# Adding partial outputs of the MLPs into y by accumulating DMAs from staging tiles, instead of by VectorE

## The chip, the core and the metric

The kernel runs on one core of a Trainium2 chip. The core has five engines with a queue of instructions each: TensorE (PE; its weight loads are listed apart as PEld), VectorE (DVE), ScalarE (ACT), GpSimd (POOL) and SyncE (SP), which here only issues DMAs. Sixteen DMA engines move the data. Matmuls write to PSUM; everything else lies in SBUF. The metric is the time of one execution on the device, in microseconds.

## The reference

A backbone of two layers over 512 latent tokens and 256 context tokens of width 1024. Each layer has a mixer (layer 0: neighbourhood attention beside spatial gating; layer 1: bidirectional retention) and then a gated MLP with a depthwise convolution over the tokens; around every sub-layer stand an RMS norm with a shift and a scale ahead of it, and a norm, a gate and the residual behind it. The change concerns the MLP:

```python
def conv_ffn(h, w_in, conv_w, conv_b, w_out):
    a = dwconv3(h @ w_in, conv_w, conv_b)          # w_in: 1024 x 5632
    gate, up = jnp.split(a, 2, axis=-1)
    return (jax.nn.silu(gate) * up) @ w_out        # w_out: 2816 x 1024

# per layer, latent stream; layer 0 also for the context stream
h = modulate(rmsnorm(x, norm_g[i, 2]), sh2, sc2)
x = x + g2 * rmsnorm(conv_ffn(h, ...), norm_g[i, 3])
```

All of it is float32.

## The kernel before

Tokens are cut into tiles of 128: tiles 0 to 3 are latent, 4 and 5 context. Layer 0 works on all six, layer 1 on the four latent ones. A float32 product is made of three passes: each operand is split into a high and a low part (`split`: ScalarE writes the high one, VectorE subtracts to get the low one, line 65), and `mm3` (lines 88 to 90) does high x high, high x low and low x high. Weights come from HBM in units of 512 KB by DMAs of SP's queue into three raw tiles, and are split into a ring of weight tiles (`unit`, `slot`).

The MLP (`ffn`) runs over 22 feature tiles j. For each, `project` multiplies the input weights of gate and up (units `f..`) with the tokens, into PSUM tiles `pf` (latent) and `pc` (context); `gated` does the convolution, the SiLU and the product on ScalarE and VectorE (lines 1148 to 1157) and splits the result into `g`. Two feature tiles are one group (`GF = 2`), and there are 11 groups. Behind every second feature tile the output projection of the group before is done: `w_out` loads and splits two units `fo..`, and `out_group` runs through the pieces. A piece is one half (512 columns) of one token tile: six matmuls into a PSUM tile `wf` (the two tiles with tag "B" are used in turn), and then the sum into y, 128 x 1024 float32 per token tile in SBUF, where layer 0's rows show it as `yf`. The first group is copied into y by ScalarE (line 389); every later one is added by VectorE (line 391):

```python
if first:
    self.S.copy(y[t][:, o], ps)
else:
    self.V.tensor_tensor(out=y[t][:, o], in0=ps, in1=y[t][:, o], op=ALU.add)
```

So a group has 12 pieces in layer 0 and 8 in layer 1. The last two groups are done by `out_last`: group A of the two early token tiles (`wf0A`, `wf1A`), then group B of these (`wf0B`), and both groups in one piece for the other token tiles (`wf0C`); B and C use the four PSUM tiles of tag "A". Behind the last piece of a token tile, `final` runs norm, gate and residual (`residual`), in which GpSimd does the roots. `ada_half` works in the background on the shifts, scales and gates of later sub-layers: GpSimd zero-fills two sums `acc` (line 199), SP loads a row into each, VectorE adds weighted rows (line 208).

Each engine takes its instructions in order. The order is fixed when the program is built, by a scheduler that places instructions by its own estimate of when they can start, and that turns every use of a tile into the needed waits on semaphores.

Of the kernel before, what the change touches and what calls it, by code (L numbers as in the profile page):

```python
# [36 lines left out]
class Trunk:  # L37
# [42 lines left out]
    def phase(self, ctx, name, extra):  # L80
        self.xp = ctx.enter_context(self.tc.tile_pool(name=name, bufs=1))
        self.extra = extra
        self.turn = 0
        return self.xp

# [42 lines left out]
    def ada_first(self, q, pool, native, tag):  # L128
        """shift and scale of a quarter of the features, latent and context, for the first sub-layer; a step per unit"""
        S, V, T = self.S, self.V, self.T  # L130
# [125 lines left out]

# [1 line left out]
    def rsq(self, w, name):  # L258
# [9 lines left out]
    def ssq(self, src, name, n):  # L268
        """mean square over the row, a half (n) at a time"""
        ss = self.sst.get(name)  # L270
        if ss is None:
            ss = self.sst[name] = self.bp.tile([P, 2], F32, name=f"ss{name}", tag="ss", bufs=8)
        junk = self.t2k(f"j{name}{n}", BF16)
        self.S.activation(junk, src, AF.Square, scale=1.0 / 32, accum_out=ss[:, n : n + 1])  # L274
# [23 lines left out]
    def residual(self, t, y, gate, src, last, name, xt):  # L298
        """y (final) -> x += rmsnorm(y) * gate; then x normed into y's place."""
        V = self.V  # L300
        self.load(xt, src)
        hv = [slice(0, 512), slice(512, 1024)]
        for n, h in enumerate(hv):
            self.ssq(y[:, h], f"y{name}{t}", n)
        for h in hv:
            V.tensor_tensor(out=y[:, h], in0=y[:, h], in1=gate[:, h], op=ALU.mult)
        r = self.rms(f"y{name}{t}")
        for n, h in enumerate(hv):
            V.scalar_tensor_tensor(out=xt[:, h], in0=y[:, h], scalar=r, in1=xt[:, h], op0=ALU.mult, op1=ALU.add)  # L309
            if last:  # L310
                self.load(self.out[t * P : (t + 1) * P, h], xt[:, h])
            else:
                self.ssq(xt[:, h], f"x{name}{t}", n)
        if last:
            return
        self.load(self.xd[t], xt)
        r = self.rms(f"x{name}{t}")
        V.tensor_scalar(out=y[:, hv[0]], in0=xt[:, hv[0]], scalar1=r, scalar2=None, op0=ALU.mult)
        self.S.activation(y[:, hv[1]], xt[:, hv[1]], AF.Copy, scale=r)
# [11 lines left out]
    def build_h(self, chunk, xn, ab, name):  # L331
        """chunk 2: context tokens, chunks 0 and 1: latent halves."""
        s = 1 if chunk == 2 else 0
# [23 lines left out]
    def hcols(self, t):  # L357
        """stationary views of token tile t: k -> (hi, lo)"""
        if t >= 4:
            c = slice((t - 4) * P, (t - 3) * P)  # L360
            return lambda k: (self.hc[0][:, k, c], self.hc[1][:, k, c])
        c = slice(t * P, (t + 1) * P)
        return lambda k: (self.hl[0][:, k, c], self.hl[1][:, k, c])

    def proj_t(self, ps, w, stream, half=None):
        """ps[feat, tokens] += w^T h, w a stationary unit"""
        h = self.hc if stream else self.hl
# [6 lines left out]

# [1 line left out]
    def out_pieces(self, feats, wo, y, toks, first, final, name, tag="B"):  # L376
        """y[t] (+)= sum over the group's feature tiles, one closure per half token tile;
        feats: list of (hi, lo)[feat, tokens]"""

        def piece(t, n):  # L380
# [7 lines left out]
            if first:  # L388
                self.S.copy(y[t][:, o], ps)
            else:  # L390
                self.V.tensor_tensor(out=y[t][:, o], in0=ps, in1=y[t][:, o], op=ALU.add)  # L391
# [9 lines left out]
    def out_last(self, A, B, y, toks, early, final, name):  # L401
        """the last two groups (feats, wo): group A of the early tokens, group B of these, both for the others"""
        e, o = toks[:early], toks[early:]
        self.out_group(*A, y, e, False, None, f"{name}A")
        if callable(B):
            B = B()
        self.out_group(*B, y, e, False, final, f"{name}B", "A")
        self.out_group(A[0] + B[0], A[1] + B[1], y, o, False, final, f"{name}C", "A")

    def finisher(self, gates, src, ab, name, xts, last=False):  # L410
        """per finished token tile: the residual update, then the next sub-layer's input once a chunk is there"""
        done = {}
# [20 lines left out]

# [1 line left out]
    def sgu(self, y, xn):  # L435
# [178 lines left out]
    def project_pair(self, j, pr):  # L614
        """q, k, v of two heads, transposed; returns the steps"""
        w = [self.unit(self.a["hyb_qkv"][(4 * i + j) * P : (4 * i + j + 1) * P], f"w{'qkv'[i]}{j}") for i in range(3)]
# [56 lines left out]
    def bias_tiles(self, h, hd):  # L673
        """8 x (relative bias, or the mask) of the three kinds of query tile"""
        G, ap = self.G, self.ap
# [13 lines left out]
    def score(self, h, b, pr, hd):  # L689
        """softmax of one query tile (b = 4: both context tiles), queries on partitions"""  # L690
        S, V, T, ap = self.S, self.V, self.T, self.ap
# [63 lines left out]
    def weigh(self, h, b, pr, hd):  # L755
        """keys onto partitions, and after a head's last tile the weighted values"""
        S, V, T = self.S, self.V, self.T
# [35 lines left out]

# [1 line left out]
    def retention(self, y, final):  # L795
        S, V, T, G, a = self.S, self.V, self.T, self.G, self.a
        KS = float(np.float32(P) ** np.float32(-0.5))
        with ExitStack() as ctx:
# [19 lines left out]
            def decay(h):  # L818
                """powers of the two decays: within a chunk, of the keys, of the queries, of a chunk"""
                d = hd[h]  # L820
# [35 lines left out]
            def k_nat(h):  # L856
                """keys onto partitions, decayed towards the end and towards the start of their chunk:
                [token tile of the chunk, direction, (context, latent), dk]"""
                d = hd[h]
# [20 lines left out]
            def states(h):  # L880
                """sums of key x value before (forwards) and behind (backwards) each chunk: [chunk, direction, dv]"""
                d = hd[h]
# [216 lines left out]

# [1 line left out]
    def ffn(self, l, y, final):  # L1101
# [192 lines left out]
def stat(w):  # L1294
    """[1024, n] -> tiles [n/128 * 128, 8 * 128]: row p of tile j holds w[k*128+p, j*128+c] as (k, c)"""
    n = w.shape[1]
# [3 lines left out]
def mov(w, width):  # L1300
    """[1024, n] -> units of 1024 / width row blocks by width columns"""
    n, g = w.shape[1], 1024 // width
# [3 lines left out]
def cols(v):  # L1306
    """[m, 1024-multiple] -> [128, ...] one column per block of 128"""
    return v.reshape(-1, P).T
# [52 lines left out]
```

## Time and profile before

| | us |
|---|---|
| median of 3 runs | 1920.09 (1918.94 to 1925.68) |
| span of the profiled execution | 1922.2 |
| TensorE busy | 1856.5 |
| VectorE busy | 1274.3 |
| ScalarE busy | 811.5 |
| GpSimd busy | 166.0 |
| MLP of layer 0, groups with adds | about 540 to 960 |
| MLP of layer 1, to the end | about 1545 to 1922 |

The span is from the first to the last instruction of one profiled execution; that execution's own time is not listed apart from its span, which lies inside the range of the runs. In a row of a group of instructions stand the line, the engine, the operation, what it writes and reads, the shape, the count, then after the bar the busy time, the mean in ns, and the idle time of the engine just before, with what ended it. In a row of a list of instructions stand the start, the duration, the engine, the line and the operation, and in brackets the idle time before. `A <- B` in a list of waits is A waiting for B: total, number, longest. Line numbers in rows of the profile are those of the kernel before; in the changed kernel lines 84 to 390 stand one further down, and later ones five.

### The profile page before, as it was taken

The page shows a single profiled execution, that of the slowest core. Times are in us where ns is not written, and L with a number is a line of the kernel's source. Part 1 is how long each engine was busy: PE and PEld are TensorE (multiplying, and loading weights), DVE is VectorE, ACT ScalarE, POOL GpSimd, SP SyncE. Part 2 cuts the span into 40 slices and gives each one's busy share as a digit, 9 for nine tenths or more (in the row PEclk, how much of TensorE's full clock was granted, in tenths as well). Part 3 has the DMA queues.
Part 4 walks back from the last instruction along what each step waited for, and adds up shares of the span by engine and source line. Part 5 has one row for each costly group of instructions (what it writes and reads, how often), then busy time and mean ns, then how long its engine had stood idle before and what let it go on. Part 6 is the DMA issues. An engine that isn't in the chain of part 4 may idle for free. (4 is left out here: it accounts for less than half of the span.)

```text
span 1922.2 us, 26580 instructions
## 1 busy us (share of the span) xinstructions
PE 1856.5 (97%) x10544; PEld 1567.6 (82%) x10544; DVE 1274.3 (66%) x2103; ACT 811.5 (42%) x1340; POOL 166.0 (9%) x249
## 2 busy tenths in 40 slices
PE   7998989989999999999989999999999899999998
PEld 4886867678888888888879889988999787888886
DVE  4844688679698755555577666676655696566565
ACT  6533545665432323222365434443444454333322
POOL 1102222130000000000021110011001100000001
PEclk9999999999999999999999999999999999999999
DMA  7323332143444311122334313331421254332222
GB/s 287 113 97 104 94 103 90 47 143 116 139 143 132 100 65 47 64 66 66 110 114 132 126 53 109 115 105 46 131 67 56 99 185 157 99 99 92 95 66 88
DMA packets 58301, 199.88 MB, mean 104 GB/s; under 512 B 7200, under 2 KB 8736, under 8 KB 58176
## 3 DMA queue, kind: packets, MB, share of 16 engines
q1 hardware_dynamic: 58176, 198.17, 31.5%
q8 instruction: 83, 1.36, 0.3%
q14 instruction: 42, 0.34, 0.1%
HBM read 187.66 MB, written 10.49 MB: 103 GB/s over the span
## 5 line engine op out<-in xcount | busy, mean ns | idle before, releaser
L208 DVE SCALAR_TENSOR_TENSOR acc<-ar,cs,acc 128x512 f32<-128x512 f32 x256 | 189.2, 759 | 21.3 <-DMA ar<-in_adaw 8.9
L391 DVE TENSOR_TENSOR yf<-wf,yf 128x512 f32<-128x512 f32 x160 | 110.0, 689 | 53.0 <-PE wf L90 52.7
L1148 ACT ACTIVATE cv<-pf,cw 128x512 f32<-128x512 f32 x88 | 67.4, 766 | 38.3 <-PE pf L90 38.2
L64 ACT ACTIVATE g<-cv 128x768 fp32r<-128x768 f32 (+1 forms) x44 | 32.6, 740 | 120.0 <-DVE cv L1157 120.0
L1149 DVE SCALAR_TENSOR_TENSOR cv<-pf,cw,cv 128x511 f32<-128x511 f32 x88 | 65.6, 745 | 16.9 <-ACT cv L1148 16.8
L1152 DVE SCALAR_TENSOR_TENSOR cv<-pf,cw,cv 128x511 f32<-128x511 f32 x88 | 65.8, 747 | 1.7
L1156 ACT ACTIVATE cv<-cv 128x768 f32<-128x768 f32 (+1 forms) x44 | 32.3, 734 | 39.4 <-DVE cv L1152 39.4
L199 POOL MEMSET acc<- 128x512 f32 x32 | 16.8, 527 | 336.8 <-DVE al L65 236.1
L1148 ACT ACTIVATE cv<-pc,cw 128x256 f32<-128x256 f32 x44 | 24.8, 564 | 49.4 <-PE pc L90 25.6
L65 DVE TENSOR_TENSOR g<-cv,g 128x768 fp32r<-128x768 f32 (+1 forms) x44 | 36.2, 822 | 12.6 <-ACT g L64 11.8
L1157 DVE TENSOR_TENSOR cv<-cv,cv 128x768 f32<-128x768 f32 (+1 forms) x44 | 36.1, 821 | 0.5
L960 DVE SCALAR_TENSOR_TENSOR of<-rx,e,of 128x256 f32<-128x256 f32 x64 | 28.9, 478 | 8.4 <-PE rx L90 7.9
L980 POOL TENSOR_SCALAR rrr<-rmv 128x2 f32<-128x2 f32 x16 | 3.1, 193 | 363.1 <-DVE rmv L977 363.1
L751 ACT ACTIVATE sc<-sc,sst 128x512 f32<-128x512 f32 x32 | 23.1, 721 | 23.1 <-DVE sc L742 22.6
L279 POOL TENSOR_SCALAR wye<-ssye 128x1 f32<-128x1 f32 x4 | 2.7, 673 | 348.3 <-ACT jye L274 348.3
L391 DVE TENSOR_TENSOR yr<-wr,yr 128x512 f32<-128x512 f32 x40 | 27.5, 688 | 5.2 <-PE wr L90 4.8
L279 POOL TENSOR_SCALAR wyc<-ssyc 128x1 f32<-128x1 f32 x6 | 4.2, 699 | 291.5 <-ACT jyc L274 291.5
L870 ACT ACTIVATE kd<-kn,e 128x256 fp32r<-128x256 f32 x32 | 14.0, 475 | 35.7 <-PE kn L867 31.5
L65 DVE TENSOR_TENSOR rv<-rn,rv 128x512 fp32r<-128x512 f32 x24 | 16.5, 686 | 18.1 <-ACT rv L64 18.1
L1149 DVE SCALAR_TENSOR_TENSOR cv<-pc,cw,cv 128x255 f32<-128x255 f32 x44 | 21.1, 479 | 9.8 <-ACT cv L1148 9.8
L986 DVE TENSOR_SCALAR on<-of,rmv,rrr 128x256 f32<-128x256 f32 x32 | 18.1, 603 | 11.8 <-POOL rrr L983 11.8
L695 PE MATMUL s<-ka,q 128*128 128x256 f32 x80 | 24.0, 321 | 1.3 <-ACT sc L708 1.1
(2836 smaller groups left out, 6928.2 us busy)
## 6 DMA issues: line engine op xcount, KB each, us to landing
ar<-in_adaw SPq DMA_DIRECT2D x96, 512.0 KB
xd<-xd SPq DMA_DIRECT2D x8, 512.0 KB
xn<-in_x SPq DMA_DIRECT2D x6, 512.0 KB
ngr<-in_norm_g SPq DMA_DIRECT2D x12, 256.0 KB
xb<-in_x SPq DMA_DIRECT2D x6, 512.0 KB
xd<-xb SPq DMA_DIRECT2D x6, 512.0 KB
xc<-xd SPq DMA_DIRECT2D x6, 512.0 KB
xd<-xc SPq DMA_DIRECT2D x6, 512.0 KB
```

The lines of the kernel that those rows point to most:

```text
L64: self.S.activation(hi, src, AF.Copy)
L65: self.V.tensor_tensor(out=lo, in0=src, in1=hi.bitcast(F32), op=ALU.subtract)
L208: V.scalar_tensor_tensor(out=acc[s], in0=raw[:, kk * 512 : kk * 512 + 512], scalar=self.cs[:, 8 * s + k : 8 * s + k + 1], in1=acc[s], op0= ...
L391: self.V.tensor_tensor(out=y[t][:, o], in0=ps, in1=y[t][:, o], op=ALU.add)
L695: T.matmul(out, q[:, cols], keys(ka), start=True, stop=False)
L751: S.activation(sc, sc, AF.Exp, bias=st[:, 0:1], scale=-1.0, accum_out=st[:, 1:2])
L960: V.scalar_tensor_tensor(out=d["o"][:, t], in0=ps[:, n], scalar=d["e"][n][:, 386 + i : 387 + i], in1=d["o"][:, t], op0=ALU.mult, op1=ALU.add,)
L1148: S.activation(d, s, AF.Identity, scale=w1, bias=b)
L1149: V.scalar_tensor_tensor(out=d[:, 1:n], in0=s[:, 0 : n - 1], scalar=w0, in1=d[:, 1:n], op0=ALU.mult, op1=ALU.add)
L1152: V.scalar_tensor_tensor(out=d[:, 0 : n - 1], in0=s[:, 1:n], scalar=w2, in1=d[:, 0 : n - 1], op0=ALU.mult, op1=ALU.add)
L1156: S.activation(act[0], act[0], AF.Silu)
L1157: V.tensor_tensor(out=act[0], in0=act[0], in1=act[1], op=ALU.mult)
```

## The change

For the two MLPs (`self.stage` is set where the pool of tiles is named "ffnp..."), a piece that is neither of the first group nor finishing its token tile is copied by ScalarE from PSUM into a staging tile `yp` of 128 x 512 float32, of which there are four, and then a DMA issued by GpSimd adds that tile to the half of y in SBUF. Pieces of the first group, pieces that finish a token tile, and the mixers stay as they were. The rest of the difference is comments.

```diff
@@ phase
         self.extra = extra
         self.turn = 0
+        self.stage = name.startswith("ffnp")
         return self.xp
@@ out_pieces
             if first:
                 self.S.copy(y[t][:, o], ps)
+            elif not final and self.stage:
+                part = self.xp.tile([P, 512], F32, name=f"yp{name}{t}{n}", tag="yp", bufs=4)
+                self.S.copy(part, ps)
+                self.G.dma_start(y[t][:, o], part, accum_op=ALU.add)
             else:
                 self.V.tensor_tensor(out=y[t][:, o], in0=ps, in1=y[t][:, o], op=ALU.add)
```

VectorE before, in a middle group of layer 0 (feature tiles 10 and 11). In a name `wf01040_6842` stand the layer (0), the first feature tile (10), the token tile (4), the half (0) and a buffer number; `fo012l` is the low part of output weight 12.

```order
L391 TENSOR_TENSOR yf004_4746<-wf01040_6842,yf004_4746 128x512
L1152 SCALAR_TENSOR_TENSOR cv0113_6817<-pf0113_6785,cw0_4004,cv0113_6817 128x511
L391 TENSOR_TENSOR yf004_4746<-wf01041_6850,yf004_4746 128x512
L1157 TENSOR_TENSOR cv0013_6810<-cv0013_6810,cv0113_6817 128x768
L391 TENSOR_TENSOR yf005_4763<-wf01050_6858,yf005_4763 128x512
```

These adds, twelve to a group, are gone from VectorE. ScalarE in the changed kernel, at the same group:

```order
L393 COPY ypf01040_6945<-wf01040_6938 128x512
L393 COPY ypf01041_6955<-wf01041_6948 128x512
L393 COPY ypf01050_6965<-wf01050_6958 128x512
L64 ACTIVATE g0013_6922<-cv0013_6906 128x768
L393 COPY ypf01051_6975<-wf01051_6968 128x512
L393 COPY ypf01000_6985<-wf01000_6978 128x512
L393 COPY ypf01001_6995<-wf01001_6988 128x512
L393 COPY ypf01010_7005<-wf01010_6998 128x512
L393 COPY ypf01011_7015<-wf01011_7008 128x512
L393 COPY ypf01020_7025<-wf01020_7018 128x512
L393 COPY ypf01021_7035<-wf01021_7028 128x512
L393 COPY ypf01030_7045<-wf01030_7038 128x512
```

Before, ScalarE had the split of `g` here and none of the copies; behind the row of the eleventh piece follow the split of output weight 12 and the twelfth copy. Each copy waits for its matmuls, and from the fifth on for the DMA that read its staging tile four copies earlier.

GpSimd in the changed kernel, where the first accumulates of layer 0 begin (`acc1..` are the sums that `ada_half` fills with zeros for layer 1):

```order
L200 MEMSET acc101_5014 128x512
L394 DMA yf004_4746<-ypf0240_5179 128x512
L200 MEMSET acc110_5457 128x512
L394 DMA yf004_4746<-ypf0241_5189 128x512
L200 MEMSET acc111_5460 128x512
L394 DMA yf005_4763<-ypf0250_5199 128x512
L394 DMA yf005_4763<-ypf0251_5209 128x512
```

Before, only the zero-fills stood in this queue; now each DMA waits there for its copy, and two zero-fills, which wait for VectorE, stand between the first three DMAs. The order of the matmuls changes only by small exchanges of neighbours, and SP's queue not at all.

## The prediction

> **What bounds the kernel now.** The page's busy times come first, then the waits of TensorE inside the two MLP stretches, then the stretches themselves.
>
> ```profile
> PE 1856.5 (97%) x10544; PEld 1567.6 (82%) x10544; DVE 1274.3 (66%) x2103; ACT 811.5 (42%) x1340; POOL 166.0 (9%) x249
> L391 DVE TENSOR_TENSOR yf<-wf,yf 128x512 f32<-128x512 f32 x160 | 110.0, 689 | 53.0 <-PE wf L90 52.7
> ```
>
> TensorE (PE) is busy 97% of the span; a pipelined PE can be busy and still be slow, so this alone proves nothing. The second row is the work that the change moves: 160 adds of 0.689 us, and what ends VectorE's idle time before them is TensorE (52.7 of 53.0 us). VectorE waits for the matmuls, not they for it. The question is then whether TensorE ever waits for VectorE here. Its waits from 440 to 970 us (MLP of layer 0), the whole list:
>
> ```profile
> PE pf L89 <- DVE hl1b L65: 0.4, 1, 0.4
> PE pf L88 <- ACT hl0b L64: 0.2, 1, 0.2
> PE wf L88 <- DVE yf L391: 0.2, 1, 0.2
> ```
>
> and from 1545 us to the end (MLP of layer 1):
>
> ```profile
> PE wf L88 <- ACT yf L389: 0.3, 1, 0.3
> ```
>
> Together 1.1 us. The stretches (columns: window, length, busy time of PE, weight loads, VectorE, ScalarE, GpSimd, then granted clock, DMA share, GB/s):
>
> ```profile
> 640.00:760.00 120.00, 119.85 (x620) 99.89 (x619) 75.16 (x110) 34.57 (x45) 0.53 (x1) 1.00 0.24 79
> 760.00:880.00 120.00, 120.00 (x635) 101.95 (x634) 66.03 (x90) 34.34 (x43) 0.00 (x0) 1.00 0.21 66
> 1600.00:1700.00 100.00, 100.00 (x432) 80.65 (x433) 61.37 (x78) 35.30 (x44) 0.00 (x0) 1.00 0.33 106
> ```
>
> Matmuls follow each other without a gap at full clock, VectorE has 40 to 45% of its time free, ScalarE some 70%, GpSimd nearly all, and the DMA engines two thirds. So the matmuls bound both MLPs, and a gain from unloading VectorE has no place to appear.
>
> **The pace of the pieces.** The rest hangs on one clock, that of a piece (half a token tile, six matmuls):
>
> ```profile
> 759.81 0.69 DVE L391 TENSOR_TENSOR yf<-wf,yf 128x512 f32<-128x512 f32 x1 [0.70 <-PE wf L90]
> 761.20 0.69 DVE L391 TENSOR_TENSOR yf<-wf,yf 128x512 f32<-128x512 f32 x1 [0.70 <-PE wf L90]
> 762.60 0.69 DVE L391 TENSOR_TENSOR yf<-wf,yf 128x512 f32<-128x512 f32 x1 [0.70 <-PE wf L90]
> ```
>
> One piece each 1.40 us ((762.60 - 759.81) / 2). A group has 12 pieces in layer 0, 8 in layer 1.
>
> **Term 1, the moved evacuation: 0.** Out go 168 adds (8 x 12 + 8 x 8 in the middle groups, 4 + 4 of the early tokens in the last): 168 x 0.689 = 116 us of VectorE. In come 168 ScalarE copies. A copy of the same shape from PSUM stands in the trace, that of the first group:
>
> ```profile
> L389 ACT COPY yf<-wf x12: 568/588/588, 490.8 to 506.5; 128x512 f32<-128x512 f32 x12
> ```
>
> 168 x 0.588 = 99 us of ScalarE, whose 811.5 become some 910: cover enough. Two PSUM buffers serve the pieces, so a buffer must be free 1.40 us after its piece ends; 0.59 does that as 0.69 did, and this first group already runs so. What can stand ahead of a copy on ScalarE is a split of a gated tile (between copies 3 and 4) or of an output weight (between 11 and 12):
>
> ```profile
> L64 ACT ACTIVATE g<-cv 128x768 fp32r<-128x768 f32 x14 | 11.9, 849 | 46.0 <-DVE cv L1157 46.0
> L64 ACT ACTIVATE fo012h<-fo012r 128x1024 fp32r<-128x1024 f32 x1 | 1.1, 1062 | 10.8 <-PE wf L90 10.8
> ```
>
> 0.85 + 0.59 = 1.44 us is 0.04 past the limit, at most; behind copy 11 no piece of the group needs a buffer any more. From 0 to 16 x 0.04 = 0.6 us: I take 0. Weights and gated tiles that ScalarE prepares behind its copies are used a whole pair of feature tiles later, and the loads have room too; SP's queue itself waits for buffers:
>
> ```profile
> SPq L50 <- DVE fo012l L65: 17.2, 1, 17.2
> ```
>
> **Term 2, the staging ring: 0, and the place where it can go wrong.** There are four staging tiles, so copy k waits until the DMA of piece k-4 has landed. Call L the time from the end of a copy to the landing. Counted from a group's start, copy 2 ends at 2 x 1.40 + 0.59 = 3.39, its DMA lands at 3.39 + L, copy 6 ends no earlier than 3.98 + L, lands at 3.98 + 2L, copy 10 ends at 4.57 + 2L, and piece 12 needs the PSUM buffer of piece 10 at 11 x 1.40 = 15.40. So a group of 12 loses nothing up to **L = 5.4 us**. In a group of 8, piece 8 needs copy 6 at 9.80: nothing up to L = 5.8.
>
> No DMA of GpSimd and no accumulating one is in this trace, so L is bounded by the nearest DMAs of SP in the chain of waits (start, duration from release to landing):
>
> ```profile
> 1563.97 3.68 DMA acc<-in_adab_row
> 1574.95 4.49 DMA fo11r<-in_ffn_out
> 1588.60 3.32 DMA f105r<-in_ffn_in
> ```
>
> A row of 2 KB takes 3.68 us, 512 KB of weights 3.32 to 4.49. The accumulate moves 256 KB, reads source and target, both on the chip. I take L = 4.1, the middle of the outer two; below 5.4. Ends: 3.3 if it behaves like the fastest; 8 if issue by GpSimd and reading the target twice over each add about as much as half a load does. L = 7 costs 4.57 + 14 - 15.40 = 3.2 us in each of 8 groups of 12 and 3.98 + 7 - 9.80 = 1.2 in each of 8 groups of 8: +35. L = 8 costs 8 x 5.2 + 8 x 2.2 = +59.
>
> Then the rate r, one DMA after another:
>
> ```profile
> q1 hardware_dynamic: 58176, 198.17, 31.5%
> ```
>
> 198.17 MB in 31.5% of 1922.2 us is 327 GB/s with all engines at work; 0.262 MB take 0.80 us, twice that if the target's reading counts fully (1.60), and 2.4 where weights take a third of the engines (share 0.33 above). A group of 12 bears 1.99 + L + 5r + 0.59 <= 15.40, with L = 4.1 that is r <= 1.74. I take 0.8 to 1.6: no stall. At r = 2.4 it is 3.3 us x 8 = +26; groups of 8 bear it (1.99 + 4.1 + 2.4 + 0.59 = 9.1 < 9.8).
>
> [...]
>
> GpSimd must also be free to issue. The longest VectorE instruction in these stretches is
>
> ```profile
> 1580.55 1.24 DVE fo11l L65
> ```
>
> If an issue had to sit out one of these, L would be 4.1 + 1.2 = 5.3, still just inside. [...]
>
> **Term 3, GpSimd's queue: +2.** A zero-fill of GpSimd stands between the first accumulates of layer 0, and waits for VectorE:
>
> ```profile
> 546.97 0.53 POOL L199 MEMSET acc<- 128x512 f32 x1 [22.30 <-DVE al L65]
> 549.79 0.53 POOL L199 MEMSET acc<- 128x512 f32 x1 [2.30 <-DVE al L65]
> 542.86 0.68 DVE L391 TENSOR_TENSOR yf<-wf,yf 128x512 f32<-128x512 f32 x1
> ```
>
> The second and third accumulate (due at 544.8 and 546.2, if copies start when the first add did, at 542.86) are held to 547.5 and 550.3, so the third lands at 554.4. Copy 7, due at 542.86 + 6 x 1.40 = 551.3, ends at 555.0 instead, and piece 9, due at 542.86 + 7 x 1.40 = 552.7, starts 2.3 us late. From 0, if VectorE with fewer adds before it frees those tiles sooner, to 3; once: +2. The other fills stand between groups, behind the last accumulate of the one and ahead of the next.
>
> **Term 4, the ends of the layers: 0.** The last VectorE adds now wait for landings of the early tokens' accumulates:
>
> ```profile
> 1892.37 0.68 DVE L391 TENSOR_TENSOR yf<-wf1A,yf 128x512 f32<-128x512 f32 x1
> 1897.73 0.69 DVE L391 TENSOR_TENSOR yf<-wf1B,yf 128x512 f32<-128x512 f32 x1 [0.67 <-PE wf1B L90]
> 1903.01 0.68 DVE L391 TENSOR_TENSOR yf<-wf1B,yf 128x512 f32<-128x512 f32 x1
> 1917.59 1.42 DVE L309 SCALAR_TENSOR_TENSOR xe<-yf,ye3r,xe 128x512 f32<-128x512 f32 x2 [0.85 <-POOL ye3r L260]
> ```
>
> First copy done at 1892.37 + 0.59, landed 4.1 later at 1897.1, before 1897.73. The tail that follows is VectorE's own and keeps its length: from -2.8 (four adds gone, 4 x 0.69) to +2.
>
> **Sum.** 0 + 0 + 2 + 0 = +2 us. The profiled execution's span is 1922.2, 2.1 above the median of 1920.09 and inside the runs (1918.94 to 1925.68), so I add to the median: **1922 us**. With the small bounds (-2.8 - 1.1 below; 0.6 + 3 + 2 above) and the runs' own spread, 1914 to 1929 for this case.
>
> **The rivals.** A measurement of this kernel tells about 0.5%, 9.6 us, from no change.
>
> 1. *The accumulates land too late* (slower). The place is ScalarE's copy, waiting for a staging tile with the PSUM buffer in its hand; it decides from L = 5.4 and costs +35 at L = 7: 1955. For it: nothing like this DMA is in the trace, and 4.49 is near. Against: 256 KB on the chip is half of the load that takes 3.3 to 4.5. Chance 0.17.
> 2. *They land one by one too slowly* (slower): the doubled reading beside weights, or GpSimd's issue itself, r = 2.4: +26, 1946; it decides from 1.74. For it: 1.60 is close below. Against: the share of 0.21 to 0.33 leaves most engines free. Chance 0.11.
> 3. *VectorE's relief shortens the changes between layers* (faster). At most the 1.1 us of waits, 2.8 at each of two layer ends, and some of the 4.8 us that TensorE lacks here:
>
> ```profile
> 980.00:1010.00 30.00, 25.21 (x170) 22.26 (x169) 22.19 (x35) 20.07 (x45) 7.37 (x12) 0.98 0.26 95
> ```
>
> That makes 1909 to 1914; against it, the work there is norms and transposes, none of which is moved. Chance 0.05.
>
> That the change does nothing is excluded: the order shows adds replaced by copies and DMAs.
>
> **How the numbers follow.** The forecast has 0.67, rivals 0.17 + 0.11 and 0.05. Faster 0.05, same 0.67, slower 0.28. The range goes down to 1913 and up to rival 1's 1955, which leaves out about 0.15.
>
> **What would show it.** Right: TensorE's waits in 520 to 880 stay near 1 us, ScalarE's copies of "yp" are released by PE, the accumulates land 3.3 to 5.4 us after their copies, VectorE's busy time falls by 116 us. Rival 1 or 2: copies released by DMA, matmuls "wf" waiting for copies, 2 to 4 us in each group of layer 0 and little in layer 1; landings a constant time late for the first, later with each piece for the second. Rival 3: the stretch 980 to 1010 shorter. The prediction is wrong if GpSimd is what the copies' DMAs wait for.

## The result and the profile after

| | before | after |
|---|---|---|
| median of the runs, us | 1919.51 (1918.78 to 1925.68, 4 runs) | 1935.05 (1933.08 to 1940.37, 4 runs) |
| ratio, 95% interval | | 1.0075 [1.0054, 1.0096] |
| span of the profiled execution, us | 1922.2 | 1934.6 |

The change costs 0.75%, about 14 us. Here is where the profiled span lost its 12.4 us, by the first matmuls of the output groups (the rows for layer 0 follow), the last matmul of layer 0 and the last of the program:

| stretch | before | after | difference |
|---|---|---|---|
| to the first moved group of layer 0 | 540.7 | 538.3 | -2.4 |
| layer 0, first moved group to the early tokens' last groups | 407.2 | 416.6 | +9.5 |
| layer 0, from there to its last matmul | 42.3 | 43.7 | +1.4 |
| layer change, mixer and first, copied group of layer 1 | 633.3 | 632.8 | -0.5 |
| layer 1, moved groups | 267.2 | 269.6 | +2.4 |
| layer 1, last matmuls | 22.0 | 22.0 | 0.0 |
| after the last matmul | 9.5 | 11.5 | +2.0 |

The first and the fourth row vary by 2 us or more from profile to profile in stretches that the change doesn't touch (the first from 537.6 to 540.7, the fourth, taken to its last copy, from 608.0 to 613.5, over six profiles); the loss is layer 0's groups, and less in the groups of layer 1 and the tail. The page of after, busy times, the two costliest new groups, the DMA queues and the issues (KB each, us from issue to landing):

```profile
PE 1856.2 (96%) x10544; PEld 1564.1 (81%) x10544; DVE 1174.7 (61%) x1935; ACT 902.0 (47%) x1508; POOL 309.9 (16%) x417
L394 POOL DMA_DIRECT2D yf<-ypf x160 | 139.3, 878 | 509.3 <-ACT ypf L393 506.7
L393 ACT COPY ypf<-wf 128x512 f32<-128x512 f32 x160 | 93.6, 585 | 106.3 <-DMA yf<-ypf 65.1
q1 hardware_dynamic: 58176, 198.17, 31.7%
q0 software_dynamic: 24192, 44.05, 13.1%
yf<-ypf POOLq DMA_DIRECT2D x160, 256.0 KB, 5.0
```

VectorE gave away 99.6 us (1274.3 to 1174.7; the 116 forecast are the sum of the single durations, which overlap their neighbours by about 0.1 us) and ScalarE took 90.5. Most of the idle time before the copies now ends with a DMA: 65.1 of 106.3 us. That is the sign that the prediction named for its two slow rivals. The list of waits says how often and how long, and who waits behind the copies:

```profile
ACT ypf L393 <- DMA yf<-ypf: 65.1, 64, 3.8
PEld wf L89 <- ACT ypf L393: 13.9, 18, 2.7
```

Sixty-four copies waited for a landing, but only 18 weight loads of TensorE waited for a copy. To see where, take the rows of the first moved groups of layer 0, and of the last one (matmuls of one line; after the durations come the first and the last start). Before:

```profile
L88 PE MATMUL wf<-fo02h,g x12: 390/396/400, 540.7 to 557.7; 128*128 128x512 f32 x12
L88 PE MATMUL wf<-fo04h,g x12: 390/396/400, 592.2 to 609.1; 128*128 128x512 f32 x12
L88 PE MATMUL wf<-fo06h,g x12: 390/396/505, 643.7 to 661.4; 128*128 128x512 f32 x12
L88 PE MATMUL wf<-fo08h,g x12: 390/396/499, 695.7 to 712.2; 128*128 128x512 f32 x12
L88 PE MATMUL wf0A<-fo018h,g x4: 390/394/396, 947.9 to 953.0; 128*128 128x512 f32 x4
```

After:

```profile
L89 PE MATMUL wf<-fo02h,g x12: 391/396/498, 538.3 to 555.6; 128*128 128x512 f32 x12
L89 PE MATMUL wf<-fo04h,g x12: 388/396/628, 592.5 to 611.9; 128*128 128x512 f32 x12
L89 PE MATMUL wf<-fo06h,g x12: 390/396/502, 648.1 to 666.7; 128*128 128x512 f32 x12
L89 PE MATMUL wf<-fo08h,g x12: 390/396/396, 702.9 to 718.2; 128*128 128x512 f32 x12
L89 PE MATMUL wf0A<-fo018h,g x4: 390/396/396, 954.9 to 959.1; 128*128 128x512 f32 x4
```

From the first to the fourth moved group: 155.0 us before (695.7 - 540.7), 164.6 after. From the fourth to the last: 252.2 before, 252.0 after. So three groups of the eight lose everything, some 2.8, 4.0 and 2.8 us, and five lose nothing at all. Windows of after over the second moved group and over the fifth (columns as in the windows of before):

```profile
592.00:618.00 26.00, 23.74 (x108) 19.30 (x108) 13.21 (x16) 11.31 (x17) 10.44 (x12) 0.93 0.94 212
754.00:772.00 18.00, 18.00 (x83) 14.58 (x82) 4.81 (x6) 10.06 (x16) 9.57 (x11) 1.00 0.84 160
```

In the group that loses, the DMA engines are busy 94% of the time and TensorE is not busy for 2.26 us; in the later group they are at 84% and TensorE has no gap. (Before, the stretch from 760 to 880 stood at 21%; the change makes that 67%, groups and what lies between them together.) The first row also has a granted clock of 0.93, and that is most of the rest of this group's 4.0 us. TensorE there:

```profile
603.30 0.50 PE L89 MATMUL wf<-fo04h,g 128*128 128x512 f32 x1 [2.26 <-ACT ypf L393]
604.32 0.63 PE L89 MATMUL wf<-fo05h,g 128*128 128x512 f32 x1
```

Behind the stall of 2.26 us the matmuls take 0.63 us instead of 0.40 and start every 0.43 us instead of every 0.23, until 607.3, at a granted clock of 0.57 (603.3 to 607.3): some 1.5 us more. The three shorter stalls in these groups (1.68, 1.29 and 1.51 us) have nothing of the kind behind them.

Now the landings, counted from GpSimd's issue, in the windows 592 to 618 and 752 to 771 (add 0.29 us, the time from a copy's end to the issue, to compare with the prediction's L):

```profile
DMA to landing us min/median/max: 4.3/6.4/9.2
...
DMA to landing us min/median/max: 4.2/4.8/5.1
```

L is 6.7 us where time is lost and 5.1 where none is: the prediction's limit of 5.4 lies between. (The twelfth accumulate of the later group, issued at 772.5, lands only after 9.0 us; no copy comes back to its tile before the next group.) ScalarE in the losing group shows a copy held 3.79 us:

```profile
598.28 0.59 ACT L393 COPY ypf<-wf 128x512 f32<-128x512 f32 x1
...
602.67 0.58 ACT L393 COPY ypf<-wf 128x512 f32<-128x512 f32 x1 [3.79 <-DMA yf<-ypf]
```

What loads the engines there stands in SP's queue, inside this group: two more weight tiles of 512 KB, background work for the modulation of layer 1. It runs beside the first groups of layer 0; its last load there is issued before 660 us.

```profile
594.82 9.73 SPq L50 DMA_DIRECT2D ar<-in_adaw  x2
```

### The profile page after: what moved, and what is told of

Its sections match the earlier page's. It is cut to its first block, busy times and chain, and to the rows that moved or that the text cites. A ratio compares the mean times of both kernels' runs of the same rounds, so it can differ in the third digit from the quotient of the medians.

```text
span 1934.6 us, 27077 instructions
## 1 busy us (share of the span) xinstructions
PE 1856.2 (96%) x10544; PEld 1564.1 (81%) x10544; DVE 1174.7 (61%) x1935; ACT 902.0 (47%) x1508; POOL 309.9 (16%) x417
## 3 DMA queue, kind: packets, MB, share of 16 engines
q0 software_dynamic: 24192, 44.05, 13.1%
## 5 line engine op out<-in xcount | busy, mean ns | idle before, releaser
L394 POOL DMA_DIRECT2D yf<-ypf x160 | 139.3, 878 | 509.3 <-ACT ypf L393 506.7
L393 ACT COPY ypf<-wf 128x512 f32<-128x512 f32 x160 | 93.6, 585 | 106.3 <-DMA yf<-ypf 65.1
L64 ACT ACTIVATE rv<-rn 128x512 fp32r<-128x512 f32 x24 | 14.2, 593 | 26.7 <-PE rn L91 26.7
L690 POOL TENSOR_TENSOR tm<-slab,mask 128x256 f32<-128x256 f32 x16 | 16.8, 1072 | 61.4 <-DVE sst L737 61.2
```

Source lines behind the costliest of these rows:

```text
L64: self.S.activation(hi, src, AF.Copy)
L393: self.S.copy(part, ps)
L394: self.G.dma_start(y[t][:, o], part, accum_op=ALU.add)
```

## The experiments

The theory after reading the two traces (theory A, the rate theory): an accumulating DMA costs the 16 DMA engines about as much time as TensorE needs for a piece, so that with any other load beside it the landings fall behind the ring of four tiles, and other loads fall behind too. From the page: q0 holds only the accumulates' bytes, 13.1% x 1934.6 us x 16 engines / 44.05 MB = 92 engine-us per MB; a piece of 0.262 MB is 92 x 0.262 / 16 = **1.51 us of all 16 engines**, and a piece comes each 1.40 us. For q1, the plain loads, the same sum gives 49.5 engine-us per MB. Rivals: the copies on ScalarE cost the time; the landing is late by its latency, not by the load; or the loss is mostly that of the weight loads running beside it. Three runs leave out or change a part of the computation; it is said with each. All edits are against the changed kernel unless said.

**The copies alone.** VectorE adds the staged copy; no DMA.

```diff
-                self.G.dma_start(y[t][:, o], part, accum_op=ALU.add)
+                self.V.tensor_tensor(out=y[t][:, o], in0=part, in1=y[t][:, o], op=ALU.add)
```

> Edit: the ScalarE copy into the staging tile stays, and VectorE adds the staging tile to y in place of the DMA. Theory A (the accumulating DMAs are late, because each takes 8 packets of 0.187 us, 1.49 us, of every DMA engine while a piece lasts 1.40 us): the three stalls in layer 0 and the late tail vanish, time 1918 to 1923, ratio to before 1.000 +- 0.002. Rival C (the copies themselves cost, since ScalarE takes them in order with its splits): the first three groups of layer 0 still lose 2 to 4 us each, time 1928 to 1935.

Measured: 1920.82 against 1921.36 us, ratio 0.9997 [0.9988, 1.0005]. Its groups of adds and copies:

```profile
L394 DVE TENSOR_TENSOR yf<-ypf,yf 128x512 f32<-128x512 f32 x160 | 110.0, 688 | 36.7 <-ACT ypf L393 35.5
L393 ACT COPY ypf<-wf 128x512 f32<-128x512 f32 x160 | 93.3, 583 | 87.3 <-PE wf L91 75.4
```

The copies and the staging tiles alone are free: without the DMAs nothing is lost. It also says that this place has nothing to give: VectorE's adds no longer hold a PSUM buffer here, and no time is saved, since TensorE waited for none.

**Six staging tiles instead of four.**

```diff
-                part = self.xp.tile([P, 512], F32, name=f"yp{name}{t}{n}", tag="yp", bufs=4)
+                part = self.xp.tile([P, 512], F32, name=f"yp{name}{t}{n}", tag="yp", bufs=6)
```

> Edit: six staging tiles instead of four. Theory A: a late landing only costs when it reaches the matmuls through the ring; with six tiles piece 12 needs the landing of piece 4, not 6, so landings up to 8.6 us are free. The three stalls in layer 0 (2.2, 4.0, 2.8 us) fall to under 1 us each, the tail stays 2 us late: 1924 to 1927. Rival D (what stalls TensorE in these groups is not the ring but late weights, because accumulates slow the loads of SP): no change, 1932 to 1937.

Measured: 1927.56, ratio 1.0033 [1.0020, 1.0045]. Copies are released by TensorE again (`PE wf`, 115 times, the first row below, from the list of waits), and the stretch of layer 0's groups is 410.3 us (before 407.2, after 416.6). Two tiles more took back 6.3 us there. The landings did not get better, they got worse (second row, window 592 to 618): counted from issue, a median of 7.7 us in the second moved group, where four tiles gave 6.4.

```profile
ACT ypf L393 <- PE wf L91: 87.3, 115, 0.9
```

```profile
DMA to landing us min/median/max: 7.2/7.7/8.0
```

A latency that is always the same would not have gone from 6.4 to 7.7 us with a deeper ring; that speaks for a queue. The time lies 0.6 us above the expected 1924 to 1927: the second and third moved groups lose nothing any more, but the first, expected to fall under 1 us, still loses 3.9, and the tail is late. A busy DMA share by itself is not what costs: in the change it is 1.07 from 607.4 to 618 and 0.98 from 906 to 928, in a later group, and TensorE is busy all of the time in both (10.60 and 22.00 us).

**Without the background loads.** In the MLPs one 512 KB tile, loaded once, is read again in place of each further weight tile of the modulation, so the modulation of layer 1 is not the reference's and those loads are left out.

```diff
+            if self.stage:
+                raw = self.kept
+            else:
                 raw = self.bp.tile([P, 1024], F32, name=f"ar{l}{half}{kp}", tag="raw", bufs=3)
                 self.load(raw, self.ada_unit_src(l, half, kp))
```

> Edit: in the MLPs the background work on shifts and gates reads one 512 KB tile that is loaded once, in place of a new weight tile for each step; these weight loads (24 of 512 KB in layer 0, 8 in layer 1) are left out, so shifts and gates of later sub-layers are not the reference's. Theory A: the first three groups of layer 0 lose their competitor on the DMA engines, landings there fall from 6.5-8.5 us to the 5.2 of the later groups, and the stalls vanish: 1923 to 1928. Rival L (a fixed latency of about 5 us from issue on GpSimd is what exceeds the ring, traffic or not): the landings stay, 1931 to 1937.

Measured: 1927.58, ratio 1.0034 [1.0022, 1.0047]. The same omission in the kernel before, as a control:

> Control for the run without the background weight loads: the same loads left out of the kernel before (adds on VectorE; shifts and gates of later sub-layers again not the reference's). Theory A: those loads cost the kernel before nothing, so its time stays: 1918 to 1924. If it is faster by 5 us or more, the gain of that other run was not the accumulates' alone.

Measured: 1916.76, ratio 0.9974 [0.9964, 0.9984], below the expected 1918 to 1924. The control matters: without it, 1927.58 looks like half of the loss removed (7.5 us of 14). But the loads cost 4 to 5 us of their own before, so the accumulates still cost 1927.58 - 1916.76 = 10.8 us where no background load runs (11.5 by the two ratios, 1.0034 / 0.9974, since the runs were taken beside different runs of the kernel before). Stretch by stretch against the control, the groups of layer 0 lose 3.9 us (410.7 against 406.9) instead of 9.5, the end of layer 0 loses 2.9, the groups of layer 1 2.1 and the tail 3.7. So the background loads are behind more than half of what layer 0's groups lose; the rest of the loss is there without them, and the copies still wait for landings 63 times (line numbers are higher in this kernel).

```profile
ACT ypf L399 <- DMA yf<-ypf: 57.2, 63, 2.7
```

**A DMA without the addition.** The same bytes by the same queue; `y` is overwritten instead of added to, so only the last group's sum arrives.

```diff
-                self.G.dma_start(y[t][:, o], part, accum_op=ALU.add)
+                self.G.dma_start(y[t][:, o], part)
```

> Edit: the same DMA of GpSimd without the addition (y is overwritten by the partial sum, so y is not the sum over the groups). Theory A: packets of 2 KB fall from 0.187 us to about 0.09, a DMA needs 0.75 us of every engine instead of 1.49, landings fall to 3.5 to 4.5 us, and the stalls vanish: 1921 to 1927. Rival L (latency of issue by GpSimd): the landings stay at 5 us and more, and the time within 3 us of the change's 1935.

Measured: 1924.51, ratio 1.0017 [1.0007, 1.0026]. Its queue and issues:

```profile
q0 software_dynamic: 13440, 44.05, 6.0%
...
yf<-ypf POOLq DMA_DIRECT2D x160, 256.0 KB, 2.9
```

6.0% x 1922.2 x 16 / 44.05 = 41.9 engine-us per MB, 0.69 us of all engines per piece: **the addition multiplies the engines' time by 2.2** (92 / 41.9), and the median landing goes from 2.9 to 5.0 us. At 0.69 us per 1.40 layer 0's groups lose 0.8 us instead of 9.5. The tail is as late as with the addition (12.1 us after the last matmul, after the change 11.5): VectorE's last instruction ends 7.7 us after the last matmul, where before it was 6.4 and after the change 8.3, and what follows takes 4.5 us instead of 3.2. So in the tail the addition is only a part of the cause; four loads of 512 KB (`xe<-xd`) are in SP's queue just there, as before and after the change. Why the end took longer here stays open.

**Layer 1 alone.**

```diff
-        self.stage = name.startswith("ffnp")
+        self.stage = name == "ffnp1"
```

> Edit: staging and accumulating DMAs in the MLP of layer 1 alone. Theory A (stalls where other weight loads meet 12-piece groups, plus a late tail): layer 1 brings some 2.6 us of short stalls and 2 us at the tail, layer 0 nothing: 1923 to 1927. Rival U (a cost per accumulate, the same everywhere): 68 of 168 moved pieces, so 0.40 of 14 us, +5.7, but without any of it at the tail.

Measured: 1925.38, ratio 1.0020 [1.0011, 1.0030]. Layer 1's moved groups take 269.0 us and the tail 11.6: +1.8 and +2.1, nearly as in the change. So layer 0 holds about 10 us of the loss and layer 1 some 4.

**The tail.** The short group of the early tokens ahead of the last one goes back to VectorE.

```diff
-            elif not final and self.stage:
+            elif not final and self.stage and not name.endswith("A"):
```

> Edit: the four early pieces of the last group of each layer (group A) go back to VectorE's adds, the rest is the change. Theory A: the last adds of VectorE no longer wait for landings of 6.7 us; the tail behind the last matmul gets its old length back, 2 to 3 us less than the change: 1930 to 1933. Rival T (the tail is late because the stalls before it moved everything): no difference to the change, 1934 to 1936, with the tail still 2 us long.

Measured: 1932.90, ratio 1.0061 [1.0045, 1.0076]; the tail is 10.1 us instead of 11.5. The two intervals overlap, so the time of 2 us is not shown by the medians alone. The mechanism is in the profile of after, on VectorE:

```profile
1908.12 0.69 DVE L396 TENSOR_TENSOR yf<-wf1B,yf 128x512 f32<-128x512 f32 x1 [2.24 <-PE wf1B L91]
1911.37 0.69 DVE L396 TENSOR_TENSOR yf<-wf1B,yf 128x512 f32<-128x512 f32 x1 [2.56 <-DMA yf<-ypf1A]
...
1929.91 1.42 DVE L310 SCALAR_TENSOR_TENSOR xe<-yf,ye3r,xe 128x512 f32<-128x512 f32 x2 [0.84 <-POOL ye3r L261]
```

The first add of the last group comes when it should, the second waits 2.56 us for the landing of the early tokens' second accumulate. All of VectorE's final work stands behind it, and ends 8.3 us after the last matmul (1923.0). With group A on VectorE the same last instruction ends 6.3 us after the last matmul (1918.6), as before the change (6.4):

```profile
1923.48 1.41 DVE L310 SCALAR_TENSOR_TENSOR xe<-yf,ye3r,xe 128x512 f32<-128x512 f32 x2 [0.84 <-POOL ye3r L261]
```

That is the whole of the 2 us on VectorE; the tail's other 0.6 us over before lie behind VectorE's last instruction.

**Both, six tiles and the tail put back.**

> Edit: six staging tiles and group A on VectorE together. Theory A: the two costs add up and go separately, so what is left is the first group of layer 0 (3 to 4 us, where landings reach 11 us): 1922 to 1926. Rival: another cost of accumulating DMAs stays at 1927 to 1930.

Measured: 1924.36, ratio 1.0013 [1.0004, 1.0023]. One wait of TensorE is left in layer 0's groups, 2.5 us in the first one, with matmuls at half pace behind it as in the second group of the change (granted clock 0.95 from 538 to 560; the group loses 4.2 us), and it is not the ring. ScalarE there:

```profile
556.41 1.06 ACT L64 ACTIVATE f017h<-f017r 128x1024 fp32r<-128x1024 f32 x1 [3.04 <-DMA f017r<-in_ffn_in]
557.38 1.05 ACT L393 COPY ypf<-wf 128x512 f32<-128x512 f32 x2
```

Two copies stand behind the split of an input weight (`f017`), and that weight comes late. Before, the same split waited even longer for its load, and it cost nothing, because the evacuations were on VectorE:

```profile
554.52 1.06 ACT L64 ACTIVATE f017h<-f017r 128x1024 fp32r<-128x1024 f32 x1 [6.40 <-DMA f017r<-in_ffn_in]
```

With the copies alone (the first experiment) the split stands at the same place and does not wait; the load is in by then:

```profile
553.87 1.07 ACT L64 ACTIVATE f017h<-f017r 128x1024 fp32r<-128x1024 f32 x1
```

So this loss needs both halves of the change: the copies put TensorE's evacuation behind the load, and the accumulates make the load late. It is issued some 10 us behind the group's first matmul in all four kernels; before, it is in 3.6 us after its issue, in the change 5.7 and here 6.4. The profile of after has it too, on ScalarE,

```profile
554.05 1.06 ACT L64 ACTIVATE f017h<-f017r 128x1024 fp32r<-128x1024 f32 x1 [2.07 <-DMA f017r<-in_ffn_in]
555.01 0.57 ACT L393 COPY ypf<-wf 128x512 f32<-128x512 f32 x1
```

and TensorE waits for that copy:

```profile
555.63 0.50 PE L89 MATMUL wf<-fo02h,g 128*128 128x512 f32 x1 [1.68 <-ACT ypf L393]
```

**Half of the pieces.** The left half of each token tile by DMA, the right by VectorE, with four tiles, and then with two (`bufs=2`).

```diff
-            elif not final and self.stage:
+            elif not final and self.stage and n == 0:
```

> Only the left half-column piece (n = 0) of each token tile goes by copy and accumulating DMA, the right one is added by VectorE; still four staging tiles. The DMA engines are then asked for 1.49 us of accumulate work per 2.80 us (two pieces) instead of per 1.40 us. Rate theory (the accumulates saturate the DMA engines): landings fall to about 4 to 5 us after the copy in all layer 0 groups, the 512 KB weight loads beside them come in time, copies wait for no DMA; layer 0's moved groups lose 0 to 2 us instead of 9.5, the tail keeps at most 2 us; 1921 to 1926. If instead each accumulate lands late whatever its rate, landings stay at 6.6 us in the second and third moved group. Four tiles would cover that here (a tile comes round only after 11.2 us), so this run tells it by the landing times, the next one by the time.

Measured: 1926.50, ratio 1.0021 [1.0011, 1.0032]. In the second moved group, then in the fourth:

```profile
DMA to landing us min/median/max: 3.3/4.0/7.6
...
DMA to landing us min/median/max: 3.3/3.3/3.7
```

At half the rate the landing falls from 6.4 to 4.0 and from 4.8 to 3.3 us (L 3.6): it hangs on the rate, and 3.3 is the shortest in both windows. No copy waits for a DMA any more. But the stretch of layer 0's groups still loses 3.2 us where 0 to 2 were expected, and the time lies half a microsecond above the expected range. VectorE in the second moved group shows how:

```profile
599.70 1.41 DVE L209 SCALAR_TENSOR_TENSOR acc<-ar,cs,acc 128x512 f32<-128x512 f32 x2 [2.58 <-DMA ar<-in_adaw]
601.03 0.68 DVE L396 TENSOR_TENSOR yf<-wf,yf 128x512 f32<-128x512 f32 x1
```

An add of a piece stood behind a step of the modulation, and that step waited 2.58 us for its background load. TensorE waits for such adds 2.9 us in these groups. It is the mechanism of `f017` on another engine:

```profile
PE wf L89 <- DVE yf L396: 2.9, 2, 2.0
```

> As the run before, but with two staging tiles instead of four, so that a tile comes round after 5.6 us, as with all pieces moved and four tiles. Rate theory: landings of 4 to 5 us, below about 5.4, so copies wait little (under 15 us in all, where the change has 65) and layer 0's groups lose 0 to 3 us: 1921 to 1927. Latency theory (each accumulate lands 6.6 us late beside weight loads, whatever the rate): the copies of the second and third moved groups wait as in the change and the time is 1928 to 1932.

Measured: 1927.80, ratio 1.0027 [1.0014, 1.0040], just outside the rate theory's 1921 to 1927 and short of the latency theory's 1928. The waits too lie between:

```profile
ACT ypf L393 <- DMA yf<-ypf: 33.2, 17, 3.8
```

33 us of waits, not under 15, and the stretch of layer 0's groups +4.4 us, not +9.5. The first one or two accumulates of the second and third moved group land up to 7.4 us after issue (L up to 7.7), behind the weight loads of 512 KB issued just ahead of them, at half the rate too. By its time this pair of runs does not separate the two theories: the landing depends on the loads that share the engines and on the accumulates' own rate. The first four landings of the second moved group, one by one, show what each does. In the change they are 7.6, 7.5, 7.4 and 7.3 us after issue; at half the rate (four tiles) 7.6, 5.9, 4.4 and 3.3; without the addition, at the full rate, 6.2, 6.1, 5.4 and 4.6. The loads ahead make the first one late whatever comes after. The change's four land 1.3 us apart, with one issued every 1.40, so the delay shrinks by only 0.1 us a piece and the ring comes round while it lasts; with half the pieces, or half the work per piece, it is worked off. (The 1.3 us also say that 1.51, the sum of the packets' times, is somewhat too long as a pace: DMA shares above 1.00, such as the 1.04 of the change from 538 to 562, show that packets' times overlap.)

**What is left when each known loss is taken away.** Six tiles; the first moved group of layer 0 and the early tokens' groups on VectorE. (148 of the 168 accumulates stay; the expectation's 140 of 160 is a slip of the count.)

```diff
-            elif not final and self.stage:
-                part = self.xp.tile([P, 512], F32, name=f"yp{name}{t}{n}", tag="yp", bufs=4)
+            elif not final and self.stage and name != "f02" and not name.endswith("A"):
+                part = self.xp.tile([P, 512], F32, name=f"yp{name}{t}{n}", tag="yp", bufs=6)
```

> Six staging tiles, and two groups go back to VectorE: the first moved group of layer 0 (whose copies stand on ScalarE behind the split of a weight that comes late) and, in both layers, the short group ahead of the last one. 140 of the 160 pieces are left on DMAs. If the losses are the ring, the weight load in the first group and the tail, and nothing else, nothing is left: 1919 to 1922, the time of before. If the accumulates cost something wherever they run, 1924 as with six tiles and the tail alone put back.

Measured: 1922.32 against 1922.59 for the kernel before in the same series, ratio 1.0001 [0.9988, 1.0013]: no loss that can be told, with 148 accumulates running.

```profile
ACT ypf L393 <- DMA yf<-ypf: 3.2, 3, 1.9
```

The DMAs are not bad wherever they run; they are bad where they come on top of other loads and where something waits for the landing. In the one profile of this kernel, an execution of 1925.94 us, the stretch of layer 0's groups was still 3.9 us longer than before, the second moved group alone 4.7. TensorE waited there for a step of the modulation:

```profile
629.97 0.40 PE L242 MATMUL at<-ident,arow 2*128 2x2 f32 x4 [2.22 <-ACT arow L239]
```

ScalarE made `arow` late because the split of an input weight ahead of it (`f0010`) had waited 11.24 us for its load; before, that split did not wait for its load. So a late load can still reach TensorE in this version. How often it does, one profile can't say. No version beats the kernel before, and TensorE's waits before, 1.1 us in both MLPs, say why hardly anything can be won by this road.

## Why the prediction was wrong in its verdict and right in its range

Forecast was no change (1922, chance 0.67), with "no change" drawn at 0.5%, and a range to 1955 for two slow rivals. Measured: slower by 0.75%, 1935.05, inside the range, between the forecast and rival 2's 1946. That the range held is in part luck: its upper end is a price for all sixteen groups, and three groups, with little in the others and at the ends, made the loss.

- **What bounds the kernel: right.** TensorE bounds both MLPs, and unloading VectorE brought nothing: with 148 adds taken off it and no loss left, the last experiment stands at 1.0001. Rival 3 did not occur. (VectorE's free share in the three stretches shown is 37 to 45%, not 40 to 45; nothing hangs on it.)
- **Term 1, the moved evacuation, 0: right as a cost, incomplete as a list of what stands ahead.** Copies in place of adds cost nothing. But the list of work that can stand ahead of a copy on ScalarE named splits of gated tiles and of output weights, and left out the split of an input weight in the first moved group, which waits for its load. In the trace of before that row stood there with 6.40 us of waiting. It cost TensorE 1.7 us in after.
- **Term 2, the staging ring, 0: the step that failed, by its sizes.** L was taken as 4.1 us, from single loads of a trace without these DMAs. It was 6.5 to 6.8 us in the first three groups of layer 0 (medians) and 5.1 to 5.4 later. The limits held: the groups of layer 0 with L up to 5.4 lost nothing, and of layer 1's groups, with a limit of 5.8, the one with L = 6.3 lost 1.3 us. With L = 6.7 the prediction's formula gives 4.57 + 2 x 6.7 - 15.40 = 2.6 us a group. The ring's stalls of the second and third group fit that: 2.26 us, and 1.29 + 1.51 us. The sum fits only by chance, 7.7 us for three groups against 9.6 measured: the first group's 2.8 us are mostly the late `f017`, and the second lost 1.5 us more at half pace behind its stall, for which the prediction has no term. The number of groups was wrong in the rival, which charged all sixteen.
- **The rate r in the same term** was taken as 0.8 to 1.6 us with no stall; measured, it is 1.3 us between queued landings, and 1.51 as the sum of the packets' times. That is within the range taken and below the limit of 1.74. What the step left out is that at a pace so near 1.40 a delay from other loads is not worked off within the group. The doubled value, 1.60, was the author's estimate for a target whose reading counts fully; no run shows the reading itself. The runs show the time: 92 engine-us per MB with the addition against 41.9 without it, a factor of 2.2. So the doubled value was the one to take, and then the question of what else is on the engines decides. There the mean share of 0.21 to 0.33 misled: it is an average over stretches of 100 us and more, while in the 26 us of a losing group accumulates and loads together reach 0.94.
- **Rivals 1 and 2 were one thing.** By the signs that the prediction gave, the second and third groups look like rival 1 (their first four accumulates all land late, after 7.6 to 7.3 and 6.6 to 6.2 us), the first like rival 2 (from 4.6 to 8.3 us within the group). In both, other loads make the delay and the rate keeps it. Rival 2 put the point at r = 1.74 with 26 us over eight groups; only the three groups with background loads beside them went over.
- **GpSimd's issuing of the DMAs** was hardly held up: the issue took 850 to 1552 ns, median 869, so the longest is 0.7 us over the median, and the list of waits has no copy waiting for GpSimd. No trace here shows an issue that sat out an instruction of VectorE, and the extra wait of 1.2 us that the prediction bounded for it is not seen.

```profile
L394 POOL DMA_DIRECT2D yf<-ypf x160: 850/869/1552, 540.8 to 1880.0; - x160
```

- **Term 3, GpSimd's queue, +2: wrong mechanism.** The zero-fill came between the first accumulates as foreseen, but it held nothing: what it waits for, two subtractions `al` of VectorE, started at 540.05 and 541.31, with no adds ahead of them. That was the lower bound given, 0.

```profile
541.54 0.85 POOL L200 MEMSET acc<- 128x512 f32 x1
542.14 1.08 POOL L394 DMA_DIRECT2D yf<-ypf  x1
```

- **Term 4, the ends of the layers, 0: the tail was +2.0, the upper bound given.** Only the first landing was reckoned (at 4.1 us; it took 4.4, in time). The second to fourth landed after some 6.7 us (L), and the second add waited. Left out of this term were r, with its doubled value, and SP's four loads of 512 KB. The addition is not the whole of it: without it VectorE still ends 1.3 us late (7.7 us against 6.4). That the loads make the rest is likely, and not shown by a run of its own. The end of layer 0 gave another +1.4; no run was made for that alone.

## What to carry to other kernels

A DMA that adds is no free adder: price its rate (here 1.51 us of all engines a piece, against 0.69 without the addition) against the pace at which pieces come (1.40), and then against what else is on the DMA engines in the same 20 us, not in the mean of a stage. Where its work is as long as the pace, a delay that other loads make hardly shrinks (here by 0.1 us a piece). Count behind a stall of TensorE what the matmuls lose afterwards, too (1.5 us behind 2.26). When evacuation moves to another engine's queue, list everything that stands ahead of it there and waits for a load; a wait that was harmless for splitting weights (6.40 us for `f017`) becomes TensorE's (1.68 us of it in the change). And before moving work off an engine, look whether anybody waits for it: here nobody did, so the best possible result was no change.

## What the hardware did that was not expected

- An accumulating DMA of 256 KB from SBUF to SBUF took 92 engine-us per MB, a plain one 41.9, and the DMAs of SP's queue 49.5. Issued each 2.8 us with no background load beside it, it lands 3.3 us after issue (median; 3.3 to 3.7), and the plain one, issued each 1.40 us there, after 2.3 (2.2 to 3.2); issued each 1.40 us beside other loads, the accumulate takes up to 10.0.
- A stall of TensorE can cost more than its length: behind 2.26 us of waiting the next matmuls ran at half pace for some 3.4 us, at a cost of 1.5 us, and behind stalls of 1.3 to 1.7 us they did not. Two runs with six tiles show it again, behind waits of 1.9 us (matmuls of 0.63 us) and 2.5 us (granted clock 0.95); the two runs with half of the pieces have waits of 2.0 us (matmuls of 0.39 to 0.40 us behind it) and 2.1 us without it. So the length alone does not decide; what does, no run here was made to tell.
- GpSimd's own time to issue differs too: 869 ns for the accumulate, 546 for the plain one. The plain one had fewer packets: less the 16 small ones of each DMA, (13440 - 168 x 16) / 168 = 64 of 4 KB, where the accumulate has (24192 - 168 x 16) / 168 = 128 of 2 KB.

```profile
L394 POOL DMA_DIRECT2D yf<-ypf x160: 536/546/777, 542.8 to 1867.0; - x160
...
DMA to landing us min/median/max: 2.2/2.3/3.2
```

(These two rows are of the DMA without the addition: its issues, and its landings in the window 702 to 720.)
